# The second feed-forward product and the second norm of a hybrid layer, laid out by token instead of by feature

## The chip, the cores and the metric

The kernel runs on one core of a Trainium2 chip. The metric is the device time of one execution in microseconds, as the median of several runs. Beside these times there is one execution taken by the hardware profiler, and a trace of it, from which all rows here come.

The engines are TensorE (PE in the rows; PEld is its weight load), VectorE (DVE), ScalarE (ACT), GpSimd (POOL) and SyncE (SP). SyncE only issues DMAs. In a matmul one operand is loaded into TensorE (it is stationary) and the columns of the other move through it; here a matmul takes 128 rows to 128 rows of the result.

## What is computed

One layer of an encoder, for two inputs that share the weights: 256 frames of a new stream ("prompt") and 64 frames of a running one ("sample"), 320 tokens of 2048 features in float32. Cut to what matters:

```python
z = x @ w_in                                  # 2048 x 7184
attn = banded softmax attention, 16 heads     # sample: with cached keys, values
h_b  = mLSTM with matrix memory, 8 heads
mix  = concat(head_norm(attn), head_norm(h_b) * sigmoid(o)) @ w_out   # 2048 x 2048
x1   = layer_norm(DN_ALPHA * x + mix, ln1_g, ln1_b)
ffn  = (silu(x1 @ w_ffn_gate) * (x1 @ w_ffn_up)) @ w_ffn_down         # 5632 wide
y    = layer_norm(DN_ALPHA * x1 + ffn, ln2_g, ln2_b)
new_k_sample = concat(cache_attn_k, k)[-512:]   # 448 old rows, 64 new; v likewise
```

The outputs are y for both inputs, the new key and value caches, and the mLSTM's states.

## The kernel before

**Products.** All weights come from memory once, in pieces of 512 KB: 128 partitions of 1024 columns (`PIECE`), which are four rows of 128 features (`nk` = 4) by 256 output columns. `load_piece` issues a piece on SyncE into one of four `raw` buffers. `split_piece` makes two parts of it for three-pass products in float32r: the high part `hi` by a cast on ScalarE (line 124), the low part `lo`, the rest, by a subtraction on VectorE (line 125); there are three buffers of each. The right-hand side (x, the mixed heads, the normed x1, the product h) is kept by feature, 128 features on the partitions and the 320 tokens along the columns, as a high and a low part too.

For each 128 output columns and each k row there are three matmuls with the weights stationary and the 320 tokens moving: `hi` with the low part (line 174), `hi` with the high part (line 175), `lo` with the high part (line 177). The result, 128 output features by 320 tokens, gathers in PSUM over all k.

**The order.** `run_plan` walks one list, `plan`: 114 pieces of `w_in`, 32 of `w_out`, then the feed-forward part in six groups of eight tiles of 128 features (the last has four). A group is eight or fewer tiles of gate and up products, written to `h` in `up_done`; the second product of a group (`down`, `down_done`) stands behind the gate and up products of the next group, that of the last group at the end. Before it multiplies piece i, `run_plan` issues loads up to piece i + 3 and splits up to piece i + 2. What else has to be done (attention, mLSTM, statistics, the first norm) is written as generators that advance by a step per piece. A scheduler then puts each engine's instructions in order; each engine works its list strictly in that order. Only the first pieces and transposes of x are ordered by hand.

**The start.** Four quarters of x are loaded in turn with the first four pieces. TensorE transposes x by tiles of 128 (line 209), ScalarE copies the high part (line 210), VectorE takes the low part (line 211), and between the transposes stand products of the first pieces. Behind them come the transposes of the parameters (lines 234 and 235) and the fifth piece. GpSimd's list has in it the copies of the old cache rows into `new_k_sample` and `new_v_sample`, 448 rows of 1024 floats each, 1.8 MB, memory to memory (line 940), and the loads of the cached keys and values for attention (lines 303 and 304) with shifted rows of the position bias (`tz`, line 312).

**The first norm.** The output product is summed onto `y`, by feature. Six transposes by TensorE (line 771) turn each 256 features to token rows, for VectorE's statistics (line 773). The first gate and up products are taken with `y * g` before the norm is known: two further columns, g and b, are carried beside the 320 tokens (322 columns), and the norm is applied to the result (`norm_product`, line 844). Meanwhile `x1_gen` makes the normed rows, by feature: per tile of 128 features a subtraction of the mean on GpSimd (line 997, into `t`), a multiplication on VectorE (line 998), a scaling and a copy on ScalarE, and the low part on VectorE (line 1001), in 16 steps.

**The second product and norm.** `down_done` adds each group's result onto `y` by feature on VectorE (line 888). In the last group each strip of 256 features is again transposed (line 771), its statistics taken (line 773), the token rows copied to `ytp` and `yts` by ScalarE (line 776) and multiplied by g on GpSimd (line 779). Behind the last product: aggregation (line 800), 1/sqrt with one step of Newton's iteration (lines 807 to 814), a product of one k row that spreads -mean r g + b, and the final `ytp * rn + that` on VectorE in twelve parts (line 1034), each followed by its DMA to the output.

## Time and profile before

| | |
|---|---|
| median of 3 runs | 1609.83 us (1607.42 to 1612.91) |
| the profiled execution (its span) | 1611.0 us |
| TensorE busy | 1579.4 us, 10906 matmuls |
| VectorE busy | 836.8 us |
| ScalarE busy | 632.3 us |
| GpSimd busy | 123.4 us |
| moved by DMA | 238.99 MB, 148 GB/s on the mean |

A busy time is the sum of an engine's instructions with overlaps counted once. TensorE's matmuls overlap (each is listed with about 0.31 us, and the next starts before it ends), so the price of one in a stream is the distance between two starts. In rows of a timeline the first number is the start in us, the second the duration; "x4" in a row joins four like instructions, and a bracket at the end gives how long the engine was idle before it and what released it. Matmuls in the trace are listed by their output and inputs: `mm<-hl,hi` is a matmul that writes a tile `mm`, from the low part of h and the high part of the weights.

### The profile page before, as it was taken

To read this page: it belongs to the slowest core of one execution; us is meant where nothing else is said; L and a number is where in the kernel's file an instruction comes from. 1 tells how busy PE (TensorE), PEld (TensorE's weight loads), DVE (VectorE), ACT (ScalarE), POOL (GpSimd) and SP (SyncE) were. 2 spreads that over 40 slices of the span, in tenths; PEclk is the share of its full clock that TensorE was granted. 3 is DMA by queue.
4 is the path that set the end of the run, shared out by engine and by line. 5 is a ranking of instruction groups with operands and counts; after the bars stand their busy time and mean duration, and the time that the engine had idled before them with its cause. 6 is when DMAs were issued, how large, how long until landed. Compare 5 with 4: busy or idle time off the path is not lost.

```text
span 1611.0 us, 26591 instructions
## 1 busy us (share of the span) xinstructions
PE 1579.4 (98%) x10906; PEld 1549.3 (96%) x10906; DVE 836.8 (52%) x1512; ACT 632.3 (39%) x972; POOL 123.4 (8%) x254
## 2 busy tenths in 40 slices
PE   5999999999999999999999999999999999999997
PEld 4999999999999999899999999999999999999996
DVE  3477585575665755853444444344444434444456
ACT  3356445444444533543333233333333333333332
POOL 3021111101000100400000000000000000000004
PEclk9999999999999999999999999999999999999997
DMA  9455444444344544354444444444444444444441
GB/s 301 152 158 153 144 144 147 149 144 128 121 128 128 176 142 143 105 169 145 151 150 148 154 145 155 145 155 146 148 153 146 156 144 154 148 150 151 148 141 66
DMA packets 225545, 238.99 MB, mean 148 GB/s; under 512 B 8683, under 2 KB 219819, under 8 KB 225227
## 3 DMA queue, kind: packets, MB, share of 16 engines
q1 hardware_dynamic: 220384, 220.23, 43.3%
q0 software_dynamic: 5040, 17.07, 3.3%
q8 instruction: 85, 1.39, 0.4%
q14 instruction: 36, 0.29, 0.1%
HBM read 230.85 MB, written 10.07 MB: 150 GB/s over the span
## 4 chain that ended last, share of the span: by engine, by line
PE 95%; DVE 2%; DMA 2%; issue 0%; ACT 0%; DVEq 0%; SPq 0%; ACTq 0%
PE mm L174 30%; PE mm L177 29%; PE mm L175 29%; DMA raw<-w_in 2%; PE w L419 1%; DVE lo L125 1%; PE w L771 1%; PE w L375 0%; PE w L399 0%; PE w L614 0%; DVE ytp L1034 0%; PE w L402 0%; PE w L352 0%; PE w L358 0%; PE w L377 0%; DVE t L998 0%
## 5 line engine op out<-in xcount | busy, mean ns | idle before, releaser
L125 DVE TENSOR_TENSOR lo<-raw,hi 128x1024 fp32r<-128x1024 f32 (+1 forms) x409 | 501.0, 1225 | 606.4 <-ACT hi L124 606.3
L124 ACT CAST hi<-raw 128x1024 fp32r<-128x1024 f32 (+1 forms) x409 | 428.1, 1047 | 754.8 <-PE mm L175 650.8
L177 PE MATMUL mm<-x1h,lo 128*128 128x320 f32 (+1 forms) x1408 | 436.5, 310 | 2.2 <-DVE lo L125 2.2
L174 PE MATMUL mm<-x1l,hi 128*128 128x320 f32 (+1 forms) x1408 | 435.6, 309 | 0.9 <-DVE np L844 0.9
L175 PE MATMUL mm<-x1h,hi 128*128 128x320 f32 (+1 forms) x1408 | 435.6, 309 | 0.0
L174 PE MATMUL mm<-xlo,hi 128*128 128x320 f32 x912 | 289.1, 317 | 0.0
L175 PE MATMUL mm<-xhi,hi 128*128 128x320 f32 x912 | 282.0, 309 | 0.0
L177 PE MATMUL mm<-xhi,lo 128*128 128x320 f32 x896 | 278.3, 311 | 0.5 <-DVE lo L125 0.5
L177 PEld LDWEIGHTS mm<-x1h,lo 128*128 128x128 f32 x1408 | 265.8, 189 | 2.6 <-DVE lo L125 2.5
L174 PEld LDWEIGHTS mm<-x1l,hi 128*128 128x128 f32 x1408 | 265.6, 189 | 1.3 <-DVE np L844 1.2
L175 PEld LDWEIGHTS mm<-x1h,hi 128*128 128x128 f32 x1408 | 265.4, 189 | 0.0
L174 PE MATMUL mm<-hl,hi 128*128 128x320 f32 x704 | 218.0, 310 | 0.0
L177 PE MATMUL mm<-hh,lo 128*128 128x320 f32 x704 | 217.5, 309 | 0.0
L175 PE MATMUL mm<-hh,hi 128*128 128x320 f32 x704 | 217.5, 309 | 0.0
L174 PEld LDWEIGHTS mm<-xlo,hi 128*128 128x128 f32 x912 | 172.4, 189 | 2.2
L175 PEld LDWEIGHTS mm<-xhi,hi 128*128 128x128 f32 x912 | 172.6, 189 | 0.0
L177 PEld LDWEIGHTS mm<-xhi,lo 128*128 128x128 f32 x896 | 169.4, 189 | 0.8 <-DVE lo L125 0.8
L175 PEld LDWEIGHTS mm<-hh,hi 128*128 128x128 f32 x704 | 132.2, 188 | 0.0
L174 PEld LDWEIGHTS mm<-hl,hi 128*128 128x128 f32 x704 | 132.1, 188 | 0.0
L177 PEld LDWEIGHTS mm<-hh,lo 128*128 128x128 f32 x704 | 132.1, 188 | 0.0
L779 POOL TENSOR_TENSOR ytp<-ytp,g 128x256 f32<-128x256 f32 x16 | 13.6, 875 | 894.6 <-ACT ytp L776 894.6
L888 DVE SCALAR_TENSOR_TENSOR y<-y,mm 128x320 f32<-128x320 f32 x96 | 46.5, 484 | 48.9 <-PE mm L177 48.6
(313 smaller groups left out, 1344.5 us busy)
## 6 DMA issues: line engine op xcount, KB each, us to landing
raw<-w_in SPq DMA_DIRECT2D x114, 512.0 KB, 3.5
raw<-w_ffn_gate SPq DMA_DIRECT2D x88, 512.0 KB, 3.5
raw<-w_ffn_up SPq DMA_DIRECT2D x88, 512.0 KB, 3.5
raw<-w_ffn_down SPq DMA_DIRECT2D x88, 512.0 KB, 3.3
raw<-w_out SPq DMA_DIRECT2D x32, 512.0 KB, 3.3
tz<-fdram POOLq DMA_DIRECT2D x16, 144.0 KB, 2.9
xq<-x_prompt SPq DMA_DIRECT2D x4, 512.0 KB, 8.6
u<-cache_attn_k POOLq DMA_DIRECT2D x4, 512.0 KB, 6.2
```

The lines of the kernel that those rows point to most:

```text
L124: S.copy(hi[:, cs], raw[:, cs])
L125: V.tensor_tensor(out=lo[:, cs], in0=raw[:, cs], in1=hi[:, cs].bitcast(F32), op=ALU.subtract)
L174: TE.matmul(o, hi[:, sl], xl, start=st, stop=False)
L175: TE.matmul(o, hi[:, sl], xh, start=False, stop=en and pc.perm)
L177: TE.matmul(o, lo[:, sl], xh, start=False, stop=en)
L419: TE.matmul(ox[r, c * 64:(c + 1) * 64], pT[0:n, j, r], src[0:n, k, v0:v0 + 64], start=(m == 0), stop=(m == len(terms[c]) - 1))
L771: TE.transpose(dst[j][:, i * P:(i + 1) * P], y[:, 2 * s + i, t0:t0 + n], ident)
L779: G.tensor_tensor(out=keep[0][:, j, cs], in0=keep[0][:, j, cs], in1=late["g2"][:, cs], op=ALU.mult)
L888: V.scalar_tensor_tensor(out=y[:, c, :], in0=y[:, c, :], scalar=ALPHA if g == 0 else 1.0, in1=ps[i][:, 0:T], op0=ALU.mult, op1=ALU.add)
```

## The change

1. **The second product by token.** The pieces of `w_ffn_down` now have two k rows and 512 output columns. `up_done` keeps h as one tile of 640 columns per feature tile: 320 high parts, 64 low parts of the sample tokens, 256 low parts of the prompt tokens. `token_products` has 128 tokens stationary and 512 weight columns moving: three matmuls for each of the two prompt tiles; two for the third tile, in which the 64 sample tokens' high and low parts stand side by side as the 128 stationary columns. Results are token rows in PSUM (rows 64 to 127 of the third tile are the low part's, added to the rest at the end).
2. **The sums by token.** `yp` and `ys` hold token rows; `stat_gen` fills them in the output product (ScalarE copies beside the statistics), and the first norm is applied to them a second time, by token, in `x1_gen`: per 512 columns and token tile a scaling on ScalarE and two passes on GpSimd, with rows of g and b loaded by `norm_rows` to all partitions (1 MB each, for ln1, later for ln2).
3. **The last group's product by token tile.** `last_down` keeps the split parts of its eight pieces and does all products of tile 0, then of tile 1, then of the sample tile. Sums and statistics follow each 512 columns (`last_sum`), the norm each tile (`last_norm`). The transposes and the one-row product of before are gone.
4. **The cache copies** stand in the source behind the first 32 pieces of the feed-forward part, not ahead of all of `run_plan`.
5. Buffers are joined: where two halves of one size stood, one of double size stands.

```diff
+    def token_products(o, j, pc, hi, lo):
+        for k in range(pc.nk):
+            wc = slice(k * 512, (k + 1) * 512)
+            h = pc.rhs(k)
+            st, en = pc.first and k == 0, pc.last and k == pc.nk - 1
+            if j < 2:
+                ts = slice(j * P, (j + 1) * P)
+                TE.matmul(o, h[:, ts], hi[:, wc], start=st, stop=False)
+                TE.matmul(o, h[:, ts], lo[:, wc], start=False, stop=False)
+                ts = slice(T + SS + j * P, T + SS + (j + 1) * P)
+                TE.matmul(o, h[:, ts], hi[:, wc], start=False, stop=en)
+            else:
+                ts = slice(SP, T + SS)
+                TE.matmul(o, h[:, ts], hi[:, wc], start=st, stop=False)
+                TE.matmul(o, h[:, ts], lo[:, wc], start=False, stop=en)
...
     def stat_gen(s):
...
+        cs = slice(s * 256, (s + 1) * 256)
+        S.copy(late["yp"][:, :, cs], pa.rearrange("p (n c) -> p n c", c=256))
+        S.copy(late["ys"][0:SS, cs], dst[2])
...
     def down_done(g, s, ps):
...
+        yp, ys = late["yp"], late["ys"]
+        cs = slice(s * 512, (s + 1) * 512)
+        for j in range(2):
+            V.tensor_tensor(out=yp[:, j, cs], in0=yp[:, j, cs], in1=ps[j], op=ALU.add)
+        V.tensor_tensor(out=ys[:, cs], in0=ys[:, cs], in1=ps[2], op=ALU.add)
...
+    def last_down():
...
+        for j in range(3):
+            ps = [mm_tile() if j != 1 else w_tile() for _ in range(4)]
+            for m, pc in enumerate(pieces):
+                if j == 0:
+                    i = n_rest + m
...
+                        split_piece(to=(slots[2 * h], slots[2 * h + 1]) if h < 7 else None)
+                    kept.append(loaded[i])
+                token_products(ps[m // 2], j, pc, *kept[m])
+                if pc.last:
+                    last_sum(j, m // 2, ps[m // 2])
+            last_norm(j)
...
+    def last_sum(j, s, ps):
...
+        V.tensor_tensor(out=y, in0=y, in1=ps[0:n, :], op=ALU.add)
+        if j == 2:
+            V.tensor_tensor(out=y, in0=y, in1=ps[SS:P, :], op=ALU.add)
+        V.bn_stats(late["st2"][0:n, j, s, :], y)
...
+    def last_norm(j):
...
+            S.activation(y, y, AF.Identity, scale=rn[0:n], bias=nb[0:n])
+            V.tensor_tensor(out=y, in0=y, in1=late["gr"][0:n, cs], op=ALU.mult)
+            add = G if j < 2 or part % 2 else V
+            add.tensor_tensor(out=y, in0=y, in1=late["br"][0:n, cs], op=ALU.add)
+            nc.sync.dma_start(out=dst[:, cs], in_=y)
...
-    for nm in ("k", "v"):
-        G.dma_start(out=O["new_%s_sample" % nm][0:PAST - SS, :], in_=I["cache_attn_" + nm][SS:PAST, :])
-
     run_plan(n_in)
...
         for part in range(4):
             cs = slice(part * 512, (part + 1) * 512)
...
+            for j, (t0, n) in enumerate(TOK):
+                v = late["yp"][:, j, cs] if j < 2 else late["ys"][0:SS, cs]
+                yield
+                S.activation(v, v, AF.Identity, scale=ra[0:n, j:j + 1], bias=nb[0:n, j:j + 1])
+                G.tensor_tensor(out=v, in0=v, in1=late["gr"][0:n, cs], op=ALU.mult)
+                G.tensor_tensor(out=v, in0=v, in1=late["br"][0:n, cs], op=ALU.add)
+        norm_rows(2)
+
+    run_plan(n_out + 32)
+
+    for nm in ("k", "v"):
+        G.dma_start(out=O["new_%s_sample" % nm][0:PAST - SS, :], in_=I["cache_attn_" + nm][SS:PAST, :])
+    run_plan(n_rest)
+    flush()
+    last_down()
```

The scheduler sets each engine's list, and the source alone doesn't tell where things land. Three places follow; line numbers behind the change are those of the changed kernel. First GpSimd at the start, behind its memsets: before,

```order
L289 MEMSET vt_86 128x3
L289 MEMSET vt_87 128x3
L940 DMA new_k_sample<-cache_attn_k 32x14336
L940 DMA new_v_sample<-cache_attn_v 32x14336
L303 DMA u_379<-cache_attn_k 128x4x256
L304 DMA u_380<-cache_attn_v 128x4x256
L312 DMA tz<-fdram 64x576 x4
```

and after (line 1093 is the copy of the cache, 332 and 333 the attention's loads, 613 loads of the mLSTM's memory):

```order
L678 MEMSET ss 128x3
L1093 DMA new_k_sample<-cache_attn_k 32x14336
L332 DMA uu<-cache_attn_k 128x4x256
L333 DMA uu<-cache_attn_v 128x4x256
L341 DMA tz<-fdram 64x576 x4
L613 DMA cn<-state_mlstm_C 128x128 x2
L1093 DMA new_v_sample<-cache_attn_v 32x14336
L341 DMA tz<-fdram 64x576
```

The copy of the keys has stayed ahead of the attention's loads; that of the values has moved behind them and behind the loads of the mLSTM's memory.

Second, the first norm by feature: GpSimd's list there is five subtractions in a row before,

```order
L997 TENSOR_TENSOR t_7276<-y,mu 128x320
L997 TENSOR_TENSOR t_7282<-y,mu 128x320
L997 TENSOR_TENSOR t_7318<-y,mu 128x320
L997 TENSOR_TENSOR t_7324<-y,mu 128x320
L997 TENSOR_TENSOR t_7360<-y,mu 128x320
```

and after, from its first subtraction (1068; 1086 and 1087 are the passes with the rows of g and b over `yp` and `ys`):

```order
L1068 TENSOR_TENSOR t_7317<-y,mu 128x320
L1068 TENSOR_TENSOR t_7323<-y,mu 128x320
L1068 TENSOR_TENSOR t_7359<-y,mu 128x320
L1086 TENSOR_TENSOR yp<-yp,gr 128x512
L1087 TENSOR_TENSOR yp<-yp,br 128x512
L1086 TENSOR_TENSOR yp<-yp,gr 128x512
L1087 TENSOR_TENSOR yp<-yp,br 128x512
L1086 TENSOR_TENSOR ys<-ys,gr 64x512
L1068 TENSOR_TENSOR t_7365<-y,mu 128x320
L1087 TENSOR_TENSOR ys<-ys,br 64x512
L1068 TENSOR_TENSOR t_7401<-y,mu 128x320
```

Six passes have come between the third and the fifth subtraction. VectorE's list at that place reads, after,

```order
L1059 SCALAR_TENSOR_TENSOR nmr<-mu,r 128x320
L1069 TENSOR_TENSOR t_7317<-t_7317,r 128x320
L1069 TENSOR_TENSOR t_7323<-t_7323,r 128x320
L1069 TENSOR_TENSOR t_7359<-t_7359,r 128x320
L1069 TENSOR_TENSOR t_7365<-t_7365,r 128x320
L1072 TENSOR_TENSOR x1l<-y,x1h 128x320 x2
L1069 TENSOR_TENSOR t_7401<-t_7401,r 128x320
L132 TENSOR_TENSOR lo<-raw,hi 128x1024
```

and before it has the same eight rows with lines 988, 998, 1001 and 125: nothing has moved there, and the low part of a weight piece stands behind the fifth multiplication in both.

Third, VectorE at the end. Before, from the sums of the last strip (888):

```order
L888 SCALAR_TENSOR_TENSOR y<-y,mm 128x320 x2
L773 BN_STATS st<-w 128x6 x4
L773 BN_STATS st<-w 64x6
L800 BN_AGGR mv<-st 128x2 x2
L773 BN_STATS st<-w 64x6
L800 BN_AGGR mv<-st 64x2
L807 TENSOR_SCALAR rnh<-mv 128x3
```

After, in the sums of the sample tile (973 and 975 add the products, 976 takes statistics, 992 multiplies by the row of g):

```order
L975 TENSOR_TENSOR ys<-ys,mm 64x512
L973 TENSOR_TENSOR ys<-ys,mm 64x512
L976 BN_STATS st_6006<-ys 64x6
L992 TENSOR_TENSOR yp<-yp,gr 128x512 x4
L975 TENSOR_TENSOR ys<-ys,mm 64x512
L973 TENSOR_TENSOR ys<-ys,mm 64x512
L976 BN_STATS st_6006<-ys 64x6
L975 TENSOR_TENSOR ys<-ys,mm 64x512
L976 BN_STATS st_6006<-ys 64x6
L981 BN_AGGR mv_15267<-st_6006 64x2
```

The strip's ten or so instructions of before have become a few per 512 columns, and the four multiplications of the second prompt tile stand between the sums of the sample tile.

## Rows read from the trace of the kernel before

**Rows 1.** The page: busy time by engine; shares of the chain that ended last.
```profile
PE 1579.4 (98%) x10906; PEld 1549.3 (96%) x10906; DVE 836.8 (52%) x1512; ACT 632.3 (39%) x972; POOL 123.4 (8%) x254
...
PE 95%; DVE 2%; DMA 2%; issue 0%; ACT 0%; DVEq 0%; SPq 0%; ACTq 0%
```

**Rows 2.** The page's groups: line, engine, operation, count; busy us, mean ns; idle before.
```profile
L174 PE MATMUL mm<-hl,hi 128*128 128x320 f32 x704 | 218.0, 310 | 0.0
```

**Rows 3.** Timeline of TensorE, second product, first and last of 25 starts: start, duration.
```profile
1530.40 0.31 PE L174 MATMUL mm<-hl,hi 128*128 128x320 f32 x1
...
1533.92 0.31 PE L174 MATMUL mm<-hl,hi 128*128 128x320 f32 x1
```

**Rows 4.** Timeline of TensorE, first gate product, 322 columns, first and last.
```profile
660.11 0.31 PE L174 MATMUL mm<-x1l,hi 128*128 128x322 f32 x1
...
663.21 0.31 PE L174 MATMUL mm<-x1l,hi 128*128 128x322 f32 x1
```

**Rows 5.** Timeline of TensorE, first products of x, lower clock, first and last.
```profile
9.98 0.47 PE L174 MATMUL mm<-xlo,hi 128*128 128x320 f32 x1
...
11.58 0.47 PE L174 MATMUL mm<-xlo,hi 128*128 128x320 f32 x1
```

**Rows 6.** Timeline of TensorE around six transposes in the last product.
```profile
1585.88 0.31 PE L177 MATMUL mm<-hh,lo 128*128 128x320 f32 x1
1586.03 0.82 PE L771 MATMUL w<-ident,y 128*128 128x128 f32 x6
...
1586.83 0.31 PE L175 MATMUL mm<-hh,hi 128*128 128x320 f32 x1
```

**Rows 7.** Timeline of TensorE behind its long stop at the start.
```profile
39.98 0.47 PE L234 MATMUL w<-ident,ra 128*128 128x128 f32 x1 [11.27 <-DVE xlo L211]
...
40.67 0.63 PE L174 MATMUL mm<-xlo,hi 128*128 128x320 f32 x1
...
44.04 0.33 PE L174 MATMUL mm<-xlo,hi 128*128 128x320 f32 x1
```

**Rows 8.** Timeline of ScalarE at the start, behind its wait for a piece.
```profile
37.23 1.04 ACT L124 CAST hi<-raw 128x1024 fp32r<-128x1024 f32 x1 [14.01 <-DMA raw<-w_in]
38.18 1.40 ACT L210 CAST xhi<-w 128x320 fp32r<-128x320 f32 x4
```

**Rows 9.** Timeline of GpSimd at the start: the copies and an attention load.
```profile
14.52 0.51 POOL L940 DMA_DIRECT2D new_k_sample<-cache_attn_k  x1
15.03 0.51 POOL L940 DMA_DIRECT2D new_v_sample<-cache_attn_v  x1
...
27.05 0.77 POOL L304 DMA_DIRECT2D u<-cache_attn_v  x1 [5.06 <-PE w L209]
```

**Rows 10.** Windows: length, PE, PEld, DVE, ACT, POOL busy; clock, DMA share, GB/s.
```profile
32.00:40.00 8.00, 0.02 (x1) 0.02 (x1) 1.70 (x3) 2.35 (x5) 0.00 (x0) 0.61 1.06 295
```

**Rows 11.** Timeline of GpSimd, two passes over 256 columns near the end.
```profile
1588.18 1.43 POOL L779 TENSOR_TENSOR ytp<-ytp,g 128x256 f32<-128x256 f32 x2 [2.05 <-ACT ytp L776]
```

**Rows 12.** Timeline of VectorE in the first norm, a low part.
```profile
664.87 1.90 DVE L125 TENSOR_TENSOR lo<-raw,hi 128x1024 fp32r<-128x1024 f32 x1
```

**Rows 13.** Timeline of TensorE, first gate and up products, start and stops.
```profile
657.80 0.41 PE L174 MATMUL mm<-x1l,hi 128*128 128x322 f32 x1
...
678.31 0.42 PE L177 MATMUL mm<-x1h,lo 128*128 128x322 f32 x1 [2.21 <-DVE lo L125]
...
684.29 0.41 PE L174 MATMUL mm<-x1l,hi 128*128 128x320 f32 x1 [0.92 <-DVE np L844]
```

**Rows 14.** Timeline behind the last product: TensorE's last matmul, then VectorE.
```profile
1590.05 0.31 PE L177 MATMUL mm<-hh,lo 128*128 128x320 f32 x1
...
1590.83 1.78 DVE L773 BATCH_NORM_STATS2 st<-w 128x6 f32<-128x256 f32 x5
...
1595.17 0.65 DVE L813 TENSOR_TENSOR rna<-rna,rnh 128x3 f32<-128x3 f32 x1
...
1604.78 2.71 DVE L1034 SCALAR_TENSOR_TENSOR yts<-yts,rn,w 64x512 f32<-64x512 f32 x4
```

More of the change, by code (lines that the diff above doesn't have):

```diff
@@ L44, with __init__ @@
 class Piece:
-    def __init__(self, src, nk, ncol, rhs, first, last, done, group, perm):
+    def __init__(self, src, nk, ncol, rhs, first, last, done, group, perm, bytok):
         self.src, self.nk, self.ncol, self.rhs = src, nk, ncol, rhs
@@ L186, in strip_pieces @@
         out = []
+        bytok = ncol == 512
         for k0 in range(0, krows, kper):
@@ L968, in x1_gen @@
     def x1_gen():
-        for _ in stat_gen(7, None):
+        for _ in stat_gen(7):
             pass
@@ L977, in x1_gen @@
         mv = norm_stats()
-        rn = norm_rsqrt(mv)
-        late["st"] = lp.tile([P, 3, 8, 6], F32, tag="st", bufs=2, name="st")
+        rn = const.tile([P, 3], F32, name="rn")
+        norm_rsqrt(mv[:, :, 1], rn, P, 3)
         yield
@@ L1027, in _build @@
-    for j, (t0, n) in enumerate(TOK):
-        v = late["ytp"][:, j, :] if j < 2 else late["yts"]
-        dst = O["y_prompt"][t0:t0 + n, :] if j < 2 else O["y_sample"]
+        ra = const.tile([P, 3], F32, name="ra1")
+        V.tensor_scalar(ra, rn, ALPHA, None, ALU.mult)
+        nb = const.tile([P, 3], F32, name="nb1")
+        V.scalar_tensor_tensor(out=nb, in0=mv[:, :, 0], scalar=-1.0, in1=ra,
+                               op0=ALU.mult, op1=ALU.mult)
+        G.tensor_scalar(late["br"], late["br"], ALPHA, None, ALU.mult)
```

182 lines of the change are left out of this document (85 added, 97 removed).

## The prediction

> **What bounds the kernel now.** I read the page first. TensorE is busy for 98% of the span and makes up 95% of the chain that ended last, so only two things move the time: the cost of one matmul in the stream, and the places where the stream stops [rows 1]. VectorE at 52%, ScalarE at 39% and GpSimd at 8% matter only at those stops.
>
> Then the timeline of TensorE, for the price of one matmul. In the second feed-forward product 24 matmuls of 320 columns start between 1530.40 and 1533.92: 146.7 ns each, where 320 columns alone at 2.4 GHz are 133.3 ns [rows 3]. At the lower clock (1.2 GHz) six starts take 1.60 us, 266.7 ns each, which is 320/1.2 and nothing more [rows 5]. The first unit has 322 columns: 21 starts in 3.10 us, 147.6 ns [rows 4]. Two more columns cost 0.9 ns, so the pitch follows the columns and is not a floor; about 13.3 ns stand on top of them at the full clock.
>
> Last, the stops. There are three. (a) The start: TensorE does nothing from 28.7 to 39.98 [rows 7]. (b) The first norm, around 676 to 684 us [rows 13]. (c) The end: the last product starts at 1590.05 and the span ends at 1611.0, 20.9 us for the second norm [rows 14].
>
> **The change part by part.**
>
> *The second product.* Before it is 3 x 704 = 2112 matmuls [rows 2], 2112 x 146.7 ns = 309.8 us. After, each k row and 512 weight columns take three matmuls for each of two token tiles and two for the third: 8 of 512 columns in place of 12 of 320. There are 44 x 4 = 176 such groups, so 1408 matmuls. In columns that is 4096 against 3840, 6.7% more; the gain can only come from paying the 13.3 ns on top 8 times and not 12. The trace has no matmul of 512 columns of this kind at the full clock, so I bound it. From below: 512/2.4 = 213.3 ns, the law of the half clock [rows 5] at the full one, with nothing on top; 300.3 us, -9.5. From above: in proportion to 320 columns, 146.7 x 1.6 = 234.7 ns; 330.4 us, +20.6. I take 13.3 ns as fixed, 226.7 ns, because 322 columns fit it (147.5 for 147.6) as they fit the upper end, and because a cost that vanishes at the half clock looks like one start-up per matmul hidden under slower columns rather than a slower read of each column. 1408 x 226.7 = 319.2 us: **+9.4 us**.
>
> The Trainium skill, page "TensorE: Matmul & The Clock Gate", section "Back-to-back issue gap", gives another law: at the full clock a start-to-start gap of columns / 2.4 plus about 2.5 ns. For 320 columns it would say 135.8 ns, and the row shows 146.7, so here it is 11 ns short [rows 3]; for 512 it would say 215.8 ns, an estimate from that page. It is a rival below.
>
> *Transposes for the second norm.* Each strip of the last product is followed by six of them. The product before starts at 1585.88, the second one behind them at 1586.83: 0.95 us where two pitches are 0.29, so 0.66 us [rows 6]. Seven of the eight sets stand in the stream: **-4.6 us**. The eighth belongs to the end.
>
> *The end.* Before: 20.9 us from the last product's start. After, only the 64 sample tokens are left when the stream ends; the two prompt tiles were normed under the products of the tile behind them (the last tile is 32 matmuls, 7.3 us). But VectorE's order puts four multiplications by g of tile 1 between the sums of the last tile, and they wait for ScalarE. Behind the last product I count on VectorE: the four (0.68 us each, by the 64x512 rows [rows 14]) 2.7, three sums at 0.68 and two statistics of 512 columns at 0.72 (twice 0.36 [rows 14]) 3.5; aggregate, root and Newton's step 2.5 (single steps took 0.65 while GpSimd ran [rows 14]); the first scaling on ScalarE 0.7; four multiplications and two additions 4.1; GpSimd's last addition sticking out by about 0.8. That is 14.3. Between the last VectorE instruction before (1607.49) and the end lie 3.5 us of transfer, which stay: 17.8. **-3 us**; from 0, if VectorE and GpSimd hold each other up all the way, to -8, if the four multiplications get done earlier.
>
> *The cache copies.* In the source they move behind the first 32 pieces of the feed-forward part, but in GpSimd's order they do not: the copy of K stands right ahead of the first attention loads, that of V only behind them and behind two loads that wait for TensorE's transposes of the parameters. So the change here is a split in time. Before, both are issued at 14.52 and 15.03 [rows 9]. ScalarE then waits 14.01 us for the fifth weight piece, until 37.23, and has behind that cast the four copies of the transposed x, for which TensorE waits 11.27 us [rows 7, 8]; in 32 to 40 us TensorE has 0.02 us of work while the DMA engines are full [rows 10]. With one copy of 1.8 MB in front and the attention loads moved behind the last transposes of x (27 us), the piece should land around 26, near the last transposes, which need no earlier copy. That takes away the 11.3 us and the slow matmuls after it: 13 starts from 40.67 to 44.04 took 3.37 us in place of 1.91, 1.5 us [rows 7]. I leave 0.8 for what remains: **-12 us**. The V copy then runs at about 33 to 38 us, when three to four pieces (3.5 us each) are in hand, and is covered; if the cover is too thin or the piece lands at 30, the clock falls again and the gain is -6. Upper end -13.
>
> *The first norm.* New here are 12 x (one ScalarE scaling, two GpSimd passes) on token rows of 512 columns. Nothing in TensorE's stream needs them before the first second product, some 150 us later, but the order puts six of the GpSimd passes between the third and the fifth subtraction of the norm by feature. On VectorE the fifth multiplication stands ahead of the low part of a weight piece, so that piece waits too. A pass over 256 columns takes 0.72 us [rows 11], 512 thus 1.43, six 8.6 us; up to 1.75 each with VectorE running beside. The low part before was done at 666.8 [rows 12]; now about 674.4. TensorE needs it in the piece that begins at 668.4 (pieces of 24 x 147.6 = 3.54 us from 657.8 on): a stop of 5.6 us and 1.5 us of slow matmuls. Against that, the stop that stands there now (678.31, 2.2 us, and the slow matmuls behind it, with 0.9 at 684.29; the unit after it begins 5.2 us late in all [rows 13]) goes, since the chain has the time to catch up. The next unit begins about 3 us later than now, and its sums and last rows come late by 2 more: **+5 us**; 0 if the slack is larger than I read, +10 if the present stop stays as well.
>
> *At no cost:* the ScalarE copies of the token rows in the output product (that engine is 39% busy [rows 1]); the low part of h in two instructions; 512-wide sums into yp and ys (VectorE is 52% busy); the row loads of g and b (2 MB twice, covered by three loaded pieces; each missing piece would cost 3.5 us); the last product's early splits, which have free buffers.
>
> **Sum.** On the profiled 1611.0: 9.4 - 4.6 - 3 - 12 + 5 = -5.2, so 1605.8. The median of the runs, 1609.83, is 1.2 below that execution: **1604.6 us**. A difference under 0.3% (4.8 us) counts as none, as no measurement of this kernel tells it from zero; so faster means below 1605.0 and slower above 1614.7, and my value lies at the edge.
>
> **The rivals.**
>
> 1. *The gap on top nearly vanishes at 512 columns.* Longer matmuls would hide the 13.3 ns as the half clock does. At 215.8 ns the product costs 303.9 us, -5.9 in place of +9.4: 1589.3. For it: the half clock's clean 266.7 [rows 5]. Against: 322 columns show no sign of it [rows 4]. The page named above is this rival's law. Chance 0.2.
> 2. *Slower: the pitch grows in proportion to the columns.* At 234.7 ns, +20.6 in place of +9.4: 1615.8. The sign turns at 1604.6 + 1.408 x (pitch - 226.7): level with before at 230.4 ns, measurably slower above 233.9. For it: 322 columns fit it too. Against: nothing of the kind at the half clock. Chance 0.12.
> 3. *The copies don't get out of the way, or the first norm stops twice.* Half the start's stop stays (+6), or +10 in place of +5 at the norm: 1609.6 to 1610.6, no change; both together 1615.6. For it: K still comes first. Chance 0.13.
>
> **How the numbers follow.** The forecast has 0.55. Its own terms (end +3/-5, start -1/+6, norm -5/+5) give about +-6 us: 0.26 below the bound of faster, 0.27 level, 0.02 slower. Rival 1 is all faster, 0.2. Rival 2: 0.05 level, 0.07 slower. Rival 3: 0.03 faster, 0.06 level, 0.04 slower. Faster 0.49, same 0.38, slower 0.13. The range reaches to rival 1 below (1588) and to rival 2 above (1616); the forecast's own is 1598 to 1611.
>
> **What would show it.** Starts 226.7 ns apart in the second product; TensorE's idle time between 28 and 40 us gone, with the fifth piece's cast near 26; a stop of 5 to 6 us near 658 (the place of 669, 12 us earlier) ended by the low part of a weight piece; about 18 us from the last product to the end. Wrong would be a pitch under 220 or over 232, a stop of over 5 us still at the start, or a stop inside the last product, where six pieces must be split ahead.

## The result, and the profile after

The changed kernel takes **1619.29 us** on the median of four runs (1618.25 to 1620.62); the kernel before, 1609.32 us on the median of four (1607.42 to 1612.91). The ratio is **1.0058, with an interval from 1.0044 to 1.0072**: 0.6% slower, 10 us. The forecast was 1604.6 with a range from 1588 to 1616; the time lies above both, and the sign is the other one. Four runs do not fix the 10 us well: in later sets of 14 to 23 runs, on two chips, the kernel before has medians of 1610.83 to 1611.60, and beside these the change would be 8 us. The changed kernel was not timed again.

The two profiled executions stand closer, 1616.5 against 1611.0. The span leaves out 1.65 to 2.1 us that the timed number has (1618.25 for the span of 1616.5). So the profiled execution of before should be the slowest of its runs (1612.91; no other lies above its span), and that of after is the fastest of its own. Of the 10 us, 5.5 are seen between the two traces; the other 4.6 are what these two lie off their medians (3.6 and 1.0). That matters below.

Cut at the first matmul of each stage, the two traces give, in us:

| stretch | before | after | difference | forecast |
|---|---|---|---|---|
| start to the end of the input product | 530.87 | 518.97 | -11.90 | -12 |
| output product | 117.29 | 117.29 | 0.00 | 0 |
| first group of gate and up products (first norm) | 233.75 | 241.18 | +7.43 | +5 |
| from there to the start of the last product's last matmul | 708.14 | 714.10 | +5.96 | +4.8 |
| from there to the end | 20.95 | 24.97 | +4.02 | -3 |
| span | 1611.0 | 1616.5 | +5.5 | -5.2 |

Two rows carry the difference between forecast and trace: the end, and less so the first norm. The page of after, busy time by engine and the chain that ended last, to be held against [rows 1]:

```profile
PE 1575.4 (97%) x10139; PEld 1494.1 (92%) x10139; DVE 864.2 (53%) x1544; ACT 649.7 (40%) x1003; POOL 170.4 (11%) x264
...
PE 84%; issue 9%; DVE 4%; POOL 1%; DMA 1%; ACT 0%; POOLq 0%; SPq 0%; ACTq 0%
```

TensorE is busy 4 us less in a span that is 5.5 us longer: on balance the loss lies where TensorE stands still. New in the chain are GpSimd and "POOLq", GpSimd's sequencer. The 9% of "issue" are nearly all two pieces (42.79 and 104.56 us, up to 645.5) in which this chain runs along GpSimd's list, while GpSimd waits for the first norm; TensorE was busy then, and no reading rests on them.

**The second product** is what was forecast. TensorE's timeline, start and duration (answers to [rows 3]):

```profile
1531.88 0.39 PE L164 MATMUL mm<-hi,hh 128*128 128x512 f32 x1
...
1535.51 0.39 PE L164 MATMUL mm<-hi,hh 128*128 128x512 f32 x1
```

That is 16 starts in 3.63 us, 226.9 ns; over whole groups (256 matmuls in 58.07 us) 226.8. The fixed 13.3 ns of the forecast said 226.7. The Trainium skill, page "TensorE: Matmul & The Clock Gate", section "Back-to-back issue gap", has columns / 2.4 and 2.5 ns more, 215.8 for these, and calls this the gap of an isolated matmul. These stand in a stream, each with weights of its own to load; the trace does not agree for them, and the measurement decides.

**The start.** TensorE runs through from the last products of x to the transposes of the parameters, where before it stood still for 11.27 us (answers to [rows 7, 8]): first ScalarE, then TensorE.

```profile
26.91 1.05 ACT L131 CAST hi<-raw 128x1024 fp32r<-128x1024 f32 x1 [3.63 <-DMA raw<-w_in]
```
```profile
29.36 0.31 PE L205 MATMUL mm<-xhi,lo 128*128 128x320 f32 x1
29.67 0.33 PE L263 MATMUL w<-ident,ra 128*128 128x128 f32 x1
```

The fifth weight piece is there at 26.91 and not at 37.23.

**The first norm.** The waits of TensorE (answers to [rows 13]), then GpSimd's and VectorE's rows that make the first of them:

```profile
662.99 0.64 PE L205 MATMUL mm<-x1h,lo 128*128 128x322 f32 x1 [5.89 <-DVE lo L132]
677.60 0.42 PE L202 MATMUL mm<-x1l,hi 128*128 128x320 f32 x1 [2.06 <-DVE np L866]
681.76 0.42 PE L202 MATMUL mm<-x1l,hi 128*128 128x320 f32 x1 [2.12 <-DVE np L866]
```
```profile
649.27 1.55 POOL L1086 TENSOR_TENSOR yp<-yp,gr 128x512 f32<-128x512 f32 x1
650.90 1.43 POOL L1087 TENSOR_TENSOR yp<-yp,br 128x512 f32<-128x512 f32 x1
652.29 1.30 POOL L1086 TENSOR_TENSOR yp<-yp,gr 128x512 f32<-128x512 f32 x1
653.66 1.29 POOL L1087 TENSOR_TENSOR yp<-yp,br 128x512 f32<-128x512 f32 x1
654.91 1.28 POOL L1086 TENSOR_TENSOR ys<-ys,gr 64x512 f32<-64x512 f32 x1
656.16 0.87 POOL L1068 TENSOR_TENSOR t<-y,mu 128x320 f32<-128x320 f32 x1
```
```profile
657.06 1.54 DVE L1069 TENSOR_TENSOR t<-t,r 128x320 f32<-128x320 f32 x1 [5.89 <-POOL t L1068]
```

Five passes of the norm by token (6.9 us) stand ahead of the fourth subtraction (656.16); VectorE waits 5.89 us for it and TensorE, behind a low part, 5.89 us too. The forecast had 5.6 for that stop, and none behind it; two of 2.1 us follow. The first 192 matmuls take 41.34 us for 36.13 before, the rest of the first group 199.83 for 197.62. VectorE has no slack there, neither before nor after. The windows show it, before and then after; behind the window stand its length and the busy times of TensorE, its weight loads and VectorE:

```profile
660.00:680.00 20.00, 17.80 (x117) 17.53 (x116) 20.00 (x24) 14.62 (x27) 14.85 (x13) 0.97 0.25 80
```
```profile
660.00:680.00 20.00, 14.60 (x82) 13.83 (x82) 20.00 (x26) 13.06 (x25) 13.28 (x11) 0.83 0.35 106
```

**The end.** VectorE and GpSimd behind the last matmul (1591.53), and the last pieces of the chain, with start and length:

```profile
1592.01 3.54 DVE L992 TENSOR_TENSOR yp<-yp,gr 128x512 f32<-128x512 f32 x4
...
1605.71 0.67 DVE L994 TENSOR_TENSOR ys<-ys,br 64x512 f32<-64x512 f32 x1
```
```profile
1592.75 6.36 POOL L994 TENSOR_TENSOR yp<-yp,br 128x512 f32<-128x512 f32 x4 [7.75 <-DVE yp L992]
1603.59 1.64 POOL L994 TENSOR_TENSOR ys<-ys,br 64x512 f32<-64x512 f32 x1 [4.47 <-DVE ys L992]
1605.86 1.64 POOL L994 TENSOR_TENSOR ys<-ys,br 64x512 f32<-64x512 f32 x1 [0.63 <-DVE ys L992]
```
```profile
1603.59 1.64 POOL ys L994
1605.23 0.59 issue
1605.83 1.68 POOLq L1127
```

The last addition ends at 1607.50, where before VectorE's last instruction ended at 1607.49, and SyncE has seen the last output land at 1610.8. Yet the span ends at 1616.5. What the program closes with on each engine (line 1127) isn't counted as busy; of it the views show only the 1.68 us of "POOLq". The trace's records have the rest: GpSimd's closing instruction, a drain, runs from 1605.83 to 1615.77, and all engines meet behind it. Before it ran from 1593.84 to 1604.82, under the last of VectorE's work.

### The profile page after: what moved, and what is told of

The parts are those of the page before. It is cut to its first block, busy times and chain, and to the rows that moved or that the text cites. A ratio compares the mean times of both kernels' runs of the same rounds, so it can differ in the third digit from the quotient of the medians.

```text
span 1616.5 us, 25082 instructions
## 1 busy us (share of the span) xinstructions
PE 1575.4 (97%) x10139; PEld 1494.1 (92%) x10139; DVE 864.2 (53%) x1544; ACT 649.7 (40%) x1003; POOL 170.4 (11%) x264
## 4 chain that ended last, share of the span: by engine, by line
PE 84%; issue 9%; DVE 4%; POOL 1%; DMA 1%; ACT 0%; POOLq 0%; SPq 0%; ACTq 0%
PE mm L202 20%; PE mm L203 19%; PE mm L205 19%; PE mm L165 5%; PE mm L167 5%; PE mm L164 5%; PE w L170 2%; PE w L171 2%; PE w L448 1%; PE w L238 1%; DVE t L1069 1%; DMA br<-ln_b 1%; DVE yp L992 1%; PE w L404 0%; DVE lo L132 0%
## 5 line engine op out<-in xcount | busy, mean ns | idle before, releaser
L131 ACT CAST hi<-raw 128x1024 fp32r<-128x1024 f32 (+1 forms) x403 | 422.2, 1048 | 716.9 <-PE mm L203 431.1
L167 PE MATMUL mm<-hi,hh 128*128 128x512 f32 x324 | 126.2, 390 | 0.0
L165 PE MATMUL mm<-lo,hh 128*128 128x512 f32 x324 | 126.2, 389 | 0.0
L164 PE MATMUL mm<-hi,hh 128*128 128x512 f32 x324 | 126.1, 389 | 0.0
L994 POOL TENSOR_TENSOR yp<-yp,br 128x512 f32<-128x512 f32 x8 | 12.7, 1612 | 860.9 <-DVE yp L992 860.9
L164 PEld LDWEIGHTS mm<-hi,hh 128*128 128x128 f32 x324 | 60.9, 188 | 12.6
L165 PEld LDWEIGHTS mm<-lo,hh 128*128 128x128 f32 x324 | 60.9, 188 | 12.5
L167 PEld LDWEIGHTS mm<-hi,hh 128*128 128x128 f32 x324 | 60.8, 188 | 12.6
L170 PE MATMUL w<-hi,hh 128*128 128x512 f32 x160 | 62.3, 389 | 0.0
```

The lines of the kernel that those rows point to most:

```text
L131: S.copy(hi[:, cs], raw[:, cs])
L164: TE.matmul(o, h[:, ts], hi[:, wc], start=st, stop=False)
L165: TE.matmul(o, h[:, ts], lo[:, wc], start=False, stop=False)
L167: TE.matmul(o, h[:, ts], hi[:, wc], start=False, stop=en)
L170: TE.matmul(o, h[:, ts], hi[:, wc], start=st, stop=False)
```

## The experiments

**The kernel before once more.** No edit.

> The kernel before, unchanged, profiled once more. Its first profile had a span of 1611.0 us, its profiled execution was the slowest of those timed (1612.91 against a median of 1609.3). Theory: what varies between executions is the stop at the start, where TensorE stood still from 28.7 to 39.98 us; a faster execution then has a stop of about 8 to 9 us and the rest of the timeline shifted by the same amount, the first norm and the end being alike within 0.5 us. Rival: the start is the same (11.3 us) and the difference of about 3 us lies somewhere else, in the first norm (5.2 us late in the first profile) or at the end (20.9 us).

Measured: 1615.06, span 1613.2. From the output product to the end nothing differs by more than 0.02 us in any stretch; the input product ends at 533.12 for 530.87. TensorE's row behind the stop, here and in a third profile of the same start (the run with a late GpSimd instruction, below, 1615.03, of which 5.8 are from its end):

```profile
41.59 0.48 PE L234 MATMUL w<-ident,ra 128*128 128x128 f32 x1 [12.40 <-DVE xlo L211]
```
```profile
35.69 0.48 PE L234 MATMUL w<-ident,ra 128*128 128x128 f32 x1 [6.92 <-DVE xlo L211]
```

The stop is 6.92, 11.27 and 12.40 us long in three executions of the same start; their input products end at 527.06, 530.87 and 533.12, and behind that only the end that was added in one of them differs. So the theory holds for these three: what varies is this stop, with the lower clock behind it. That the whole spread of the kernel before (1607 to 1616) lies there is likely, and not shown, since its fastest and slowest executions were not traced.

**The last additions on VectorE.**

```diff
-            add = G if j < 2 or part % 2 else V
+            add = G if j < 2 else V
```

> The changed kernel with one difference: the last two of the four additions of b for the sample tile, which were GpSimd's, are VectorE's. In the changed kernel the last output row has landed at about 1610.8, and the span ends at 1616.5; GpSimd's closing instruction of the program (a drain) ran from 1605.83 to 1615.77, 8.3 us beyond GpSimd's last addition (1607.50). In the kernel before it ended at 1604.8, 8.3 us behind GpSimd's last multiplication (1596.5), under VectorE's work. Theory: the drain ends some 8.3 us behind GpSimd's last instruction, whatever else runs. Then GpSimd's last addition is that of the second prompt tile, done at 1599.1, its drain ends at 1607.4, and the end is set by VectorE: four multiplications and four additions of 0.68 us from 1601.5, 1607.0, and 3.5 us behind it, 1610.5: 6 us less than the changed kernel, about 1613.5 on the median. Rival 1: the drain takes as long, but counted from the end of the other engines' work; then nothing is gained, or the time is 1 us longer for VectorE's longer chain. Rival 2: only the two GpSimd additions' own overhang counts: 1 us less.

Measured: 1613.27, a ratio of 1.0011 to the kernel before (1.0001 to 1.0021), where the changed kernel had 1.0058: 7.6 us by the ratios. In the trace the end takes 18.50 us for 24.97, 6.5 less. (The first group took 1.5 us more in this execution, 242.68, which nothing here explains.) GpSimd's last addition ends at 1600.10, its drain at 1608.36, 8.3 us behind, and no longer sets the end. The theory holds, both rivals fall.

**GpSimd's passes held behind its subtractions.**

```diff
-        G.tensor_scalar(late["br"], late["br"], ALPHA, None, ALU.mult)
+        tc.keep_in_program_order(G.tensor_scalar(late["br"], late["br"], ALPHA, None, ALU.mult))
...
-                G.tensor_tensor(out=v, in0=v, in1=late["gr"][0:n, cs], op=ALU.mult)
+                tc.keep_in_program_order(G.tensor_tensor(out=v, in0=v, in1=late["gr"][0:n, cs], op=ALU.mult))
```

> The changed kernel with GpSimd's 24 passes of the norm by token, and the scaling of the row of b, held behind the last of its 16 subtractions of the norm by feature. VectorE's list is the same as in the changed kernel. There the fourth subtraction waits for five passes (649.3 to 656.2), VectorE for 5.9 us on it, a low part of a weight piece behind VectorE, and TensorE 5.89 us on that at 662.99; then TensorE waits 2.06 and 2.12 us for the norm of the first products. The first gate and up products and the rest of the first group take 241.2 us in the changed kernel, 233.8 in the one before. Theory: the six passes make this difference; pinned, the stop of 5.9 us goes and that of before (2.2 and 0.9 us) comes back: 7.4 us less, about 1612 on the median. Rival: VectorE is the bound there, with 20 us of work in 20 us; the stop of 5.9 only moves, into the waits for the norm of the first products, and the gain is 1 to 3 us.

Measured: 1625.31, a ratio of 1.0090 (1.0071 to 1.0110); neither theory nor rival, 5 us slower than the changed kernel. The stop of 5.9 us did go (0.43 is left of it), and the first 192 matmuls took 33.99 us for 41.34. But the rest of the first group took 212.72 for 199.83. TensorE's two longest waits there, then GpSimd's scaling and VectorE's rows beside it:

```profile
678.09 0.63 PE L202 MATMUL mm<-x1l,hi 128*128 128x320 f32 x1 [5.00 <-DVE np L866]
688.51 0.46 PE L205 MATMUL mm<-x1h,lo 128*128 128x320 f32 x1 [2.88 <-DVE lo L132]
```
```profile
671.80 5.60 POOL L1079 TENSOR_SCALAR br<-br 128x2048 f32<-128x2048 f32 x1
```
```profile
668.00 0.48 DVE L1072 TENSOR_TENSOR x1l<-y,x1h 128x320 fp32r<-128x320 f32 x1
...
672.10 4.33 DVE L1072 TENSOR_TENSOR x1l<-y,x1h 128x320 fp32r<-128x320 f32 x2
...
679.04 2.30 DVE L132 TENSOR_TENSOR lo<-raw,hi 128x1024 fp32r<-128x1024 f32 x1
```

A low part of x1 takes 0.48 us at 668.00, where GpSimd is idle. Beside GpSimd's 5.6 us scaling two of them take 4.33, of which 3.93 are the first. The low part of a weight piece takes 2.30 beside a pass, and 1.21 at 668.81. VectorE is busy 59.1 us of the 60 from 645 on (48.8 in the changed kernel, where it stands still for 5.9). The Trainium skill, page "SBUF — State Buffer", section "Who interferes with whom", says that a VectorE instruction with two inputs in SBUF contends with a GpSimd instruction that reads SBUF, for ports that one of them holds at a time. The rows agree that the two hold each other up, though not for the whole of GpSimd's row: by the trace's records VectorE's second low part and the three multiplications behind it took 0.48 us each from 675.95 on, and the scaling's row ends at 677.40. So the passes have two prices: one in GpSimd's own order, and one in VectorE's time, and this edit traded the first for the second. (It also moved the scaling, which in the changed kernel lies early: a mistake of the edit, and a part of the 13 us; how large a part is not shown.)

**The norm by token later.** In `x1_gen` the 24 passes become a generator of their own, started by the second pair of gate tiles; the scaling of b stays early.

```diff
+    def tok_norm():
+        ra, nb, keep = late["ra"], late["nb"], tc.keep_in_program_order
...
             hbuf[("sg", 2 * u + i)] = sg
+        if u == 1:
+            spawn(late["tok"](), 1)
```

> The changed kernel with the norm by token (scalings on ScalarE, passes on GpSimd) started by the second pair of gate tiles, some 80 us later, where VectorE is busy for 40% and no chain waits. The scaling of the row of b stays early. When the passes were only held behind the 16 subtractions, the first products got faster by 7.4 us (33.99 for 41.34), but the rest of the first group slower by 12.9: GpSimd's passes then ran beside VectorE's busiest stretch, and VectorE's operations with two operands in SBUF took 2.3 us and more for 1.2 (a pair of low parts 4.33 for 0.88 us beside GpSimd's 5.6 us scaling). Theory: GpSimd and VectorE hold each other up, and away from that stretch the passes cost nothing: the first 192 products take about 34 us, the rest of the group about 198, 9 us less than in the changed kernel in all, about 1610 where that had 1619, level with the kernel before. Rival: VectorE's own work is the bound there; 232 us stay out of reach, and the sum is 238 to 241.

Measured: 1612.50, a ratio of 1.0005 (0.9994 to 1.0016), 8.5 us less than the changed kernel by the ratios. The first pass now starts 56 us behind the first gate product, where it was 13: some 43 us later, not the 80 expected. First group: 36.09 and 197.61, 233.70 us, the kernel before to 0.05. TensorE's first wait is that of before again:

```profile
669.74 0.42 PE L205 MATMUL mm<-x1h,lo 128*128 128x322 f32 x1 [2.16 <-DVE lo L132]
```

The theory holds in its sum (233.7 for 241.2); that the first products would be faster than before (34 us) did not come. That gain belonged to the order of the run before this one; why, no run shows.

**The copies at their old place, in the changed kernel.** The loop of the two copies stands ahead of `run_plan(n_in)` again.

> The changed kernel with both copies of the old cache rows at their old place, ahead of all attention loads. Theory: TensorE's stop of some 8 to 11 us at the start and the lower clock behind it come back, and with them the 11.9 us by which the changed kernel's input product ends earlier in the first profile: 1627 to 1631 on the median. Rival: the shift came from another thing that changed at the start (buffers joined, the attention loads' place); then the time stays at 1619.

Measured: 1625.71, a ratio of 1.0090 (1.0073 to 1.0107): 5 us more than the changed kernel by the ratios, less than the 8 to 12 expected. The stop came back, at less than half its length in the first profile:

```profile
34.88 0.33 PE L263 MATMUL w<-ident,ra 128*128 128x128 f32 x1 [4.87 <-DVE xlo L240]
```

In the traces the input product ends 6.6 us later than in the changed kernel, and nothing behind it differs. The load of the cached keys was issued at 28.35 here, at 21.20 in the kernel before, since the buffers are joined. That this makes the stop shorter is not shown: the stop of the kernel before alone varies from 6.92 to 12.40, and with both copies held back (the next pair of runs) that load, issued at 22.14, makes no stop. What is shown is that without the copies there is none.

**The copies moved, in the kernel before**, as the change moves them (first edit), and held on GpSimd behind its other work (second):

```diff
-    run_plan(len(plan))
+    run_plan(n_out + 32)
+    for nm in ("k", "v"):
+        G.dma_start(out=O["new_%s_sample" % nm][0:PAST - SS, :], in_=I["cache_attn_" + nm][SS:PAST, :])
+    run_plan(len(plan))
```
```diff
-        G.dma_start(out=O["new_%s_sample" % nm][0:PAST - SS, :], in_=I["cache_attn_" + nm][SS:PAST, :])
+        tc.keep_in_program_order(G.dma_start(out=O["new_%s_sample" % nm][0:PAST - SS, :], in_=I["cache_attn_" + nm][SS:PAST, :]))
```

> The kernel before with one part of the change alone: the two cache copies stand in the source behind the first 32 pieces of the feed-forward part. In GpSimd's order the copy of the keys stays ahead of the first attention loads and that of the values goes behind them, as in the changed kernel. With the copies put back, the changed kernel's input product ended 6.6 us later (525.60 against 518.97). Theory: the copies' place alone is worth 6 to 7 us, and the other part of the 11.9 us of the first profile is the later load of the cached keys (joined buffers), some 2 to 3 us, and the spread of the kernel before between executions. Then this one takes 5 to 8 us less than the kernel before. Rival: the copies are all of it, 9 to 12 us less.

> The kernel before with both copies held behind all that GpSimd has to do up to the first 32 pieces of the feed-forward part, so that they run some 100 us behind the first norm, beside a steady stream of weight pieces. Theory: the start has only the loads that attention needs; TensorE's stop goes wholly, as in the changed kernel (the input product ends near 519 to 520), and the copies cost nothing where they are: 8 to 11 us less than the kernel before. Rival 1: the stop that is left is made by the load of the cached keys, 5 us; then 5 us less. Rival 2: 3.7 MB of copies take the DMA engines from the weight pieces where they now run and TensorE stops there for several us; then no gain.

Measured: 1602.79 and 1602.29 beside 1610.83 for the kernel before, ratios 0.9946 (0.9934 to 0.9958) and 0.9945 (0.9932 to 0.9959): 8.7 and 8.9 us less. By the ratios this is a little over what the first theory gave for the split (5 to 8; the medians differ by 8.0), and within that for the hold (8 to 11). TensorE's timeline of the two: a short stop is left with the split; none with the hold, which pays with two waits behind the first norm:

```profile
30.85 0.33 PE L234 MATMUL w<-ident,ra 128*128 128x128 f32 x1 [2.18 <-DVE xlo L211]
```
```profile
687.72 0.41 PE L174 MATMUL mm<-x1l,hi 128*128 128x320 f32 x1 [1.10 <-ACT hi L124]
688.98 0.41 PE L177 MATMUL mm<-x1h,lo 128*128 128x320 f32 x1 [0.70 <-DVE lo L125]
```

**Three mends together.** The changed kernel with the norm by token late, the last additions on VectorE, and the copies held on GpSimd.

> The changed kernel with three things mended: the norm by token late, the last two additions on VectorE, and both copies held behind GpSimd's other work. Theory: 9 us and 6 us less than the changed kernel, and nothing more from the copies, since the stop at the start was gone already: 15 us less, 0.6% of the time under the kernel before (about 1603 to 1605 where that has 1610 to 1611). Rival: the gains overlap, or the copies disturb the stream where they now run; then it is level with the kernel before.

Measured: 1611.57 (1606.45 to 1613.66), a ratio of 0.9999 (0.9989 to 1.0009): level, as the rival had it. The profiled execution is the fastest of them: span 1604.8, end 18.86 us, first group 236.4 us with 1.43 and 0.70 us of waits where the copies run (761 to 763). What made the other eleven executions 3 to 7 us slower than this one no trace shows. They have a lower mean granted clock, 0.992 to 0.994 for 0.995; a longer stop beside the copies would give that, and so would a late rise of the clock at the start (last section). The last pair below bears on it.

**Matmuls in halves.** Each of 512 columns as two of 256.

```diff
-                TE.matmul(o, h[:, ts], hi[:, wc], start=st, stop=False)
+                for q in range(2):
+                    oc, w2 = o[:, q * 256:(q + 1) * 256], slice(k * 512 + q * 256, k * 512 + (q + 1) * 256)
+                    TE.matmul(oc, h[:, ts], hi[:, w2], start=st and q == 0, stop=False)
```

> The changed kernel with each matmul of 512 weight columns in the second product made as two of 256, in the same order of operands: 2816 in place of 1408, the same columns in all. In the changed kernel the 512 columns started 226.7 ns apart, the 320 of the other products 146.7. Theory: 13.3 ns stand on top of columns / 2.4 GHz once per matmul; then 256 columns start 120.0 ns apart, the product takes 337.9 us for 319.2, and the time rises by 18.7 us. Rival: the time on top grows with the columns (6% of them); then 113.3 ns, and the time stays.

Measured: 1636.93 in one run, 17.6 us over the changed kernel's median; the stretch with the second product is 18.1 us longer (732.23 for 714.10). Starts:

```profile
1540.13 0.28 PE L166 MATMUL mm<-hi,hh 128*128 128x256 f32 x1
...
1541.57 0.28 PE L166 MATMUL mm<-hi,hh 128*128 128x256 f32 x1
```

12 starts in 1.44 us, 120.0 ns. The rival falls: 256, 320 and 512 columns have 13.3, 13.3 and 13.5 ns on top of columns / 2.4.

**One small GpSimd instruction behind the end of the kernel before.**

```diff
             nc.sync.dma_start(out=dst[:, cs], in_=v[0:n, cs])
+    G.tensor_copy(eps[0:SS, :], late["yts"][0:SS, DM - 1:DM])
```

> The kernel before with one instruction more: GpSimd copies one column of 64 values of the sample rows behind VectorE's last operation. In the kernel before GpSimd's last work ended at 1596.5 and its closing drain at 1604.8, before the last output had landed. Theory: the drain ends 8.3 us behind GpSimd's last instruction, however small; here that is at about 1607.7, the drain ends at 1616.0 and the span 0.75 us later, 1616.8 for 1611.0: 5.8 us longer. Rival: the drain's time depends on the work in GpSimd's queue (its passes over 256 and 512 columns), and one small copy costs nothing or a few tenths of a us.

Measured: 1617.21, a ratio of 1.0036 (1.0024 to 1.0048), 5.8 us more. GpSimd's row:

```profile
1603.79 0.18 POOL L1037 COPY eps<-yts 64x1 f32<-64x1 f32 x1 [11.14 <-DVE yts L1034]
```

It ends at 1603.97; the drain's record ends at 1612.31, 8.3 us behind, and the span at 1613.1. From the last product's last matmul to the end it is 26.87 us for 20.95. The theory holds: not GpSimd's work but its last instruction starts the 8.3 us.

**The copies apart, in the kernel before and in the mended one.** The copies become 14 of 64 rows on SyncE, one behind every fourth piece; the second kernel has the late norm and VectorE's additions besides.

```diff
+    for i in range(14):
+        run_plan(n_out + 48 + 4 * i)
+        nm, r = "kv"[i // 7], i % 7 * 64
+        tc.keep_in_program_order(
+            nc.sync.dma_start(out=O["new_%s_sample" % nm][r:r + 64, :],
+                              in_=I["cache_attn_" + nm][SS + r:SS + r + 64, :]))
```

> The kernel before with the two cache copies cut into 14 of 64 rows (256 KB), issued on SyncE between the weight pieces, one for every four pieces from the 48th piece of the feed-forward part on. With the copies held on GpSimd they ran right behind the first norm, where three loaded pieces were not in hand, and TensorE stopped for 1.1 and 0.7 us there (the rest of the first group took 199.95 us for 197.62). Theory: apart, they cost nothing; about 2 us less than with the copies held on GpSimd (1602.3), 11 us less than the kernel before. Rival: on SyncE's queue each copy stands ahead of a weight piece, and the pieces come late by about 1 us each; if the three pieces in hand do not cover that, TensorE stops up to 14 times, and the time is some us longer than 1602.

> The changed kernel with the norm by token late, the last two additions on VectorE, and the copies in 14 parts on SyncE as in the run before with the product by feature. So the two differ in the second product, the sums and the second norm alone. By the traces the product by token is 9.4 us longer in matmuls and 3.9 us shorter for transposes; from the last matmul to the end it takes 18.9 us (the changed kernel with the additions on VectorE) for 20.9. Theory: 3.5 us more than the product by feature, and 7 to 8 us less than the kernel before. Rival: they are level, if the passes by token cost nothing and more of the end is hidden.

Measured: 1601.73 by feature, ratio 0.9940 (0.9925 to 0.9955), and 1605.09 by token, 0.9961 (0.9948 to 0.9975), beside 1611.23 for the kernel before. The copies cost nothing in TensorE's stream now (first group 233.7 us in both, as before), and the two differ by 3.4 us where the terms said 3.5; beside the kernel before, the one by token gains 6.3 us by the ratio and not the 7 to 8 expected. By token is the slower one. The fastest version here is the kernel before with its copies apart, 9.5 us or 0.6% faster than before and 1.2% faster than the changed kernel. Its lead over the copies split or held (ratios 0.9946 and 0.9945) is within the intervals, so the 2 us expected of it are not shown; its profiled execution had the late rise of the clock. The kernel by token is 6.1 us faster, by the ratios, with the copies apart than with them held on GpSimd, more than the 2.7 us of that one's trace. That large copies beside the stream have a price that varies from one execution to the next would fit this, and is not shown.

## Why the prediction was wrong, step by step

The forecast was 14.7 us too low; as a change it was -5.2 where +10.0 was measured. Of the signs it named, three came: the starts 226.8 ns apart, the fifth piece's cast at 26.91, and a stop of 5.89 us at the place of the first norm. The fourth, about 18 us from the last product to the end, did not: it was 25.0. Its own steps, against what was measured:

*The second product, +9.4: right.* The fixed 13.3 ns held at 512 columns, and the halves set it apart from a share of the columns. Rivals 1 and 2 both fell by this. The second product has 6.7% more columns for four matmuls fewer in twelve, and that is a loss.

*Transposes, -4.6: nearly.* Six sets stood in the stream before, not seven, since the seventh comes behind the last product as well: -3.9. With the product the trace has +5.96 to the last matmul for the +4.8 forecast, some 0.4 us of it from other things.

*The first norm, +5: the first stop right, the size off by 2.4.* The stop was 5.89 for 5.6. Wrong was that the later stop would go because "the chain has the time to catch up": it has none. VectorE is busy there without a gap (20 us of 20 from 660 on), and was so before, which the trace of before shows; so what VectorE lost in the stop it could not catch up, and TensorE waited twice more. The unit behind the first one began 5.2 us later than before (41.34 for 36.13), for the 3 of the forecast; the 2 us for what follows came as 2.2. Holding GpSimd's passes back where they stand made it worse, starting them 43 us later removed the whole +7.4.

*The start, -12: the mechanism right, the size too large by 3 to 5.* The stop went, and the traces show 11.9; that this is so near the forecast is luck at both ends. The term was taken from an execution whose stop was 11.27 us long; others had 6.92 and 12.40. And the profile of after caught no stop at all, where other executions with the same start had 0.22, 0.59 and 2.12 us (the additions on VectorE, the passes held, the halves). Taking the medians, 10.0 in all less the other three differences (7.4, 6.0 and 4.0) leaves -7.4; with the later medians of before it is about -9. The copies alone, in the kernel before, are -8.7. The sign that this was a long one stood in the table: I set the span of 1611.0 against the median of 1609.83 and called the difference 1.2, though a span is some 1.9 us shorter than the time of its run in this kernel. So the profiled execution was 3 us slow. The step that failed is taking the whole stop of that execution as a term and setting the sum against the median of the runs, whose stops were shorter.

*The end, -3: wrong by 7, and the largest miss.* VectorE's and GpSimd's rows took 1.7 us more than forecast: the last of them ends at 1607.50, 16.0 us behind the last product for the 14.3 of the sum (17.4 before), and the outputs have landed 19.3 us behind it. The step that failed is "GpSimd's last addition sticking out by about 0.8": what sticks out is 8.3 us of drain behind that addition, and it puts the end of the span at 1616.5, where 1607.50 and the 3.5 us of before would have given 1611. The runs show it from three sides, taken away (-6.5), added to the kernel before with 0.18 us of work (+5.9), and hidden in before, where the drain ended at 1604.8.

Together: 4.6 (start) + 7.0 (end) + 2.4 (norm) + 1.2 (product and transposes) are the 15.2 between -5.2 and +10.0. With the later medians of before, the change is some 8 us and the start's part of this 3. Of rival 3 one half came true: the first norm did stop more than once, at 7.4 us for its 10. The other half, a stop left at the start, was not in the profile. Both halves together gave 1615.6, and what goes beyond comes from the end, for which the forecast gave a range of 0 to -8: it counted the work of VectorE and GpSimd, and had no term for what the program does behind it.

## What to carry to other kernels

Before a term is taken from one trace, set its run's time against the spread of the others, like with like, and ask in which stop that spread lies. At the end of this program no GpSimd instruction should stand in the last 9 us; VectorE's 0.68 us is cheaper there than GpSimd's 1.64 and what follows it. A product that trades more columns for fewer matmuls pays here columns / 2.4 ns and 13.3 ns for each matmul, and work for GpSimd beside a busy VectorE can cost VectorE time too, or make it wait.

## What the runs showed of the hardware

- GpSimd's closing drain ends 8.3 us behind GpSimd's last instruction: 8.26 or 8.34 us in twelve of fourteen traces, behind passes of 0.71 to 1.64 us and behind a copy of 0.18 us alike, and 8.17 and 8.09 in the two kernels whose cache copies SyncE issues.
- Float32r matmuls at the full clock start columns / 2.4 and 13.3 to 13.5 ns more apart: 120.0, 146.7 and 226.8 ns for 256, 320 and 512 columns. At the lower clock nothing stands on top [rows 5].
- In two of fourteen traces TensorE's matmuls came to the full clock (2.4 GHz) at 22 us, in the others at 15 to 17, with the same list of work (55 matmuls ahead of it for 37). The start was about 3 us longer: the input product ends at 522.33 for 518.97 in the two kernels shown. Starts in one of each kind, the mended norm's kernel and the changed one, where the distance goes from 0.27 to 0.15 us:

```profile
21.83 0.47 PE L205 MATMUL mm<-xhi,lo 128*128 128x320 f32 x1
22.09 0.41 PE L202 MATMUL mm<-xlo,hi 128*128 128x320 f32 x1
22.34 0.31 PE L203 MATMUL mm<-xhi,hi 128*128 128x320 f32 x1
```
```profile
15.93 0.41 PE L202 MATMUL mm<-xlo,hi 128*128 128x320 f32 x1
16.18 0.31 PE L203 MATMUL mm<-xhi,hi 128*128 128x320 f32 x1
```
